# The S5 gate of a hybrid decoder trunk: last block's GELU behind the heads' Sigmoids, unfolding by two engines, gate products of the last block last

## The chip, the cores and the metric

One Trainium2 chip, one core. The metric is the device time of one execution, in microseconds, as the median of three runs. PE is TensorE, DVE VectorE, ACT ScalarE, POOL GpSimd, SP the queue that issues most DMAs.

## The reference

The reference is a decoder trunk of two layers, 512 positions by 1024 channels. The change lies in layer 0, whose mixer has two parallel parts behind one input projection: S5 (512 channels, a complex diagonal recurrence) and HGRN2 (four heads of 128 channels, gated linear attention). Cut to what matters:

```
z = h @ ev_w_in;  u, hq, hf, hi, hg = split(z)
# S5: states over time, then
y   = gelu(Re(C @ states) + d * u)                 # 512 x 512
y_a = y * sigmoid(y @ w_glu + b_glu)               # the S5 gate
# HGRN2, per head
query = silu(hq); forget = lb + (1 - lb) * sigmoid(hf); key = (1 - lb) * sigmoid(-hf)
o   = chunk_gated_linear(query, key, hi, log(forget))
y_b = rms_norm(o) * silu(hg)
mixed = concat(y_a, y_b) @ ev_w_out
```

Then come the residual, a norm with modulation, a SwiGLU FFN, and a second layer with gated linear attention (GLA), another FFN and the last norm. All is float32.

## The kernel before, in words

**Number format.** A float32 product is made of three products of a high and a low part: `split` (line 258) and `wsplit` (line 246) write a high part on ACT and the rest, a difference, on DVE. `proj` (line 269) issues three matmuls for each block of 128 input channels into one PSUM tile of 128 x 512.

**S5.** The 512 channels are four blocks of 128. `s5_block` (line 768) works one block: ACT folds the block so that four time steps share a column (`U`), PE projects it (`vps`), DVE and POOL rotate and scan (`rz...`), and PE forms the output `yp`: for each of four groups j three matmuls of 128 columns (each is recorded as two passes). The output is still folded. Line 813 unfolds it with 16 ACT copies, one for each j and each of four time steps, from 32 partitions of `yp` to every fourth column of `yf`.

**Gate.** `gelu` (line 1080) applies the function to all four `yf`. `s5_glu` (line 816) loads and splits the gate's weights, splits the four `yf` into `yr`, and for each of four output tiles makes 12 matmuls into `ps`, in the order of the input blocks, then a Sigmoid on ACT, a product with `yf` on POOL and a split. Its results `ys` are the first four input blocks of the output projection `out_first` (line 885, tiles `op`).

**Heads.** `hg_fq` (line 1031) projects query and forget gate of one head (`hq`, `hf`); their Sigmoids, and DVE's product for the query (line 1046), read the PSUM tiles. `hg_g` (line 1055) does the output gates of two heads (`hg`). `core` (line 444) is the recurrence of one head in seven levels (`dgp`, `lv`), `hg_outs` norms and gates the heads' outputs (`y_h`).

**PSUM.** Eight banks: four buffers `mm` (`mm_ps`), two `a`, two `b` (`ps_a`, `ps_b`). Buffers of one kind go round in program order; a new tile waits until all readers of the one that had its buffer are done. Head 3's `hq` and `hf`, the two `hg` tiles and then the four gate tiles take the four `mm` buffers in this order. `vps`, `yp` and the fold of the modulation (`ada_run`, line 192, `fold`) use `b`.

**What sets the order.** The program is written in one order (lines 1084 to 1104). A planner with a model of the engines then fixes each engine's queue; it can put work that is written later ahead of work that would wait. ACT's functions with tables are the exception: `tact` (line 91) chains them in program order and puts a table load where the set changes (`sigmoid`, `gelu` and others are different sets). Copies and Squares are in every set. The modulation of later stages is summed on DVE step by step (`ada_run`), with its weights loaded on SP.

Of the kernel before, what the change touches and what calls it, by code (L numbers as in the profile page):

```python
# [13 lines left out]
AF = mybir.ActivationFunctionType  # L14
# [3 lines left out]
P = 128  # L18
D = 1024
T = 512  # L20
# [21 lines left out]
def trunk(  # L42
# [10 lines left out]
    out = out[0]  # L53
# [11 lines left out]
    def tt(name, tag, shape=(P, T), dtype=F32):  # L65
        return tp.tile(list(shape), dtype, tag=tag, name=name, bufs=SLOTS[tag])
# [7 lines left out]
    def mm_ps(name, shape=(P, T)):  # L74
        return pm.tile(list(shape), F32, tag="mm", name=name)

    def ps_a(name, shape=(P, T)):
        return pa.tile(list(shape), F32, tag="a", name=name)

    def ps_b(name, shape=(P, T)):  # L80
        return pa.tile(list(shape), F32, tag="b", name=name)

    V, A, G, PE = nc.vector, nc.scalar, nc.gpsimd, nc.tensor

    def act(o, i, f, **kw):
        return A.activation(out=o, in_=i, func=f, **kw)  # L86
# [4 lines left out]
    def tact(o, i, f, **kw):  # L91


        def queue(new):
            if table["last"] is not None:
                tc.add_manual_dep(new.ins, table["last"].ins.name, order, reason="table sets in order")
            table["last"] = new

        if table["set"] != TABLES[f]:
            table["set"] = TABLES[f]  # L100
            queue(A.preload_act_table_set(TABLES[f]))
        ins = act(o, i, f, **kw)
        queue(ins)
        return ins

    def ttv(e, o, a, b, op):
        e.tensor_tensor(out=o, in0=a, in1=b, op=op)  # L107
# [133 lines left out]
    def wraw(src, nk, name, cols=P):  # L241
        raw = wp.tile([P, nk, cols], F32, tag="raw", name=f"raw_{name}", bufs=3)
        nc.sync.dma_start(out=raw, in_=src.rearrange("(k p) n -> p k n", p=P))
        return raw

    def wsplit(raw, nk, name, cols=P, e=nc.vector):
        hi = wp.tile([P, nk, cols], F32R, tag="whi", name=f"whi_{name}", bufs=3)
        act(hi, raw, AF.Copy)
        lo = wp.tile([P, nk, cols], F32R, tag="wlo", name=f"wlo_{name}", bufs=3)
        ttv(e, lo, raw, hi.bitcast(F32), ALU.subtract)  # L250
        return hi, lo
# [6 lines left out]
    def split(e, src, name, th, tl):  # L258
        hi = tt(f"hi_{name}", th, dtype=F32R)
        lo = tt(f"lo_{name}", tl, dtype=F32R)  # L260
        act(hi, src, AF.Copy)
        ttv(e, lo, src, hi.bitcast(F32), ALU.subtract)
        return hi, lo
# [5 lines left out]
    def proj(ps, ws, acts, ts=slice(0, T), ks=None):  # L269

        n = len(ws)
        for i, ((hi, lo), (ah, al)) in enumerate(zip(ws, acts, strict=True)):
            if ks and i not in ks:
                continue
            PE.matmul(ps, lhsT=hi, rhs=ah[:, ts], start=(i == 0), stop=False)  # L275
            PE.matmul(ps, lhsT=hi, rhs=al[:, ts], start=False, stop=False)  # L276
            ins = PE.matmul(ps, lhsT=lo, rhs=ah[:, ts], start=False, stop=(i == n - 1))  # L277
        return ins
# [238 lines left out]
    def in_step(*runs):  # L517

        runs = list(runs)
        while runs:  # L520
            runs = [r for r in runs if next(r, runs) is not runs]
# [246 lines left out]
    def s5_block(q, uT, mats, rot):  # L768

        rho = prm[3]  # L770
        Km, Wn, (Wr, Wi) = mats
        cosT, sinT = rot
        shp = [P, 4, P]
        U = tt(f"U{q}", "X" if q < 3 else "s", (P, 4, P))
        for j in range(4):
            for s in range(4):
                r = 3 - s
                act(U[32 * r : 32 * r + 32, j, :], uT[32 * j : 32 * j + 32, s:T:4], AF.Copy)
        vps = []
        for i in range(2):  # L780
            ps = ps_b(f"vps{q}{i}", (P, 4, P))
            for j in range(4):
                PE.matmul(ps[:, j, :], lhsT=Wn[i][:, j, :], rhs=U[:, j, :], start=True, stop=True)
            vps.append(ps)
        t = [tt(f"rz{q}{z}", "s", shp) for z in "abcd"]
        ttv(V, t[0], vps[0], cosT, ALU.mult)
        ttv(V, t[1], vps[1], sinT, ALU.mult)
        ttv(V, t[2], vps[1], cosT, ALU.mult)
        ttv(V, t[3], vps[0], sinT, ALU.mult)
        ttv(V, t[0], t[0], t[1], ALU.add)  # L790
        ttv(G, t[2], t[2], t[3], ALU.subtract)
        z = [t[1], t[3]]
        for i in range(2):
            for j in range(4):
                V.tensor_tensor_scan(
                    out=z[i][:, j, :], data0=rho[:, q * 4 + j : q * 4 + j + 1].to_broadcast([P, P]),
                    data1=t[2 * i][:, j, :], initial=0.0, op0=ALU.mult, op1=ALU.add)

        ttv(V, t[0], z[0], cosT, ALU.mult)
        ttv(G, t[2], z[1], sinT, ALU.mult)  # L800
        ttv(V, t[0], t[0], t[2], ALU.subtract)
        ttv(V, z[0], z[0], sinT, ALU.mult)
        ttv(G, z[1], z[1], cosT, ALU.mult)
        ttv(V, z[0], z[0], z[1], ALU.add)
        yp = ps_b(f"yp{q}", (P, 4, P))
        for j in range(4):
            PE.matmul(yp[:, j, :], lhsT=Km[:, j].rearrange("p t c -> p (t c)"), rhs=U[:, j, :], start=True, stop=False)
            PE.matmul(yp[:, j, 1:], lhsT=Wr[:, j, :], rhs=t[0][:, j, 0 : P - 1], start=False, stop=False)
            PE.matmul(yp[:, j, 1:], lhsT=Wi[:, j, :], rhs=z[0][:, j, 0 : P - 1], start=False, stop=True)
        yf = tt(f"yf{q}", "r")  # L810
        for j in range(4):
            for s in range(4):
                act(yf[32 * j : 32 * j + 32, s:T:4], yp[32 * s : 32 * s + 32, j, :], AF.Copy)
        return yf

    def s5_glu(yf):
        wg = []
        for i in range(2):
            w = wsplit(wraw(s5_w_glu[0, i * 2 * P : (i + 1) * 2 * P, :], 2, f"wg{i}", T), 2, f"wg{i}", T, V)
            wg += [tuple(z[:, k, :] for z in w) for k in range(2)]  # L820
        yr = [split(V, y, f"yr{k}", "s", "s") for k, y in enumerate(yf)]
        res = []
        for m in range(4):
            ps = mm_ps(f"glu{m}")
            proj(ps, [tuple(z[:, m * P : (m + 1) * P] for z in w) for w in wg], yr)
            y = tt(f"ys{m}", "s")
            tact(y, ps, AF.Sigmoid, bias=cols2[:, 12 + m : 13 + m])
            ttv(G, y, y, yf[m], ALU.mult)
            res.append(split(V, y, f"ys{m}", "s", "s"))
        return res  # L830
# [119 lines left out]
    for m in range(KT):  # L950
        ps = mm_ps(f"xps{m}")
# [10 lines left out]
    for m in range(KT):  # L962
        ps = (mm_ps if m < 4 else ps_b)(f"xnps{m}")
# [29 lines left out]
    for i in range(2):  # L993
        w = split(V, raw[3][:, 4 * i : 4 * i + 4, :].rearrange("p k n -> p (k n)"), f"u3{i}", "t", "t")
# [19 lines left out]
    def tok_tiles(src, name, f, tag):  # L1014

        os = [tt(f"{name}{i}s", tag, (P, 2, 2 * P)) for i in range(2)]
        f(os, proj_tok(src, h, name))
        return os
# [36 lines left out]
    def hg_g(pr):  # L1055
        c0 = S5W + 3 * 512 + pr * 2 * P
        return tok_tiles(win[:, c0 : c0 + 2 * P], f"hg{pr}", hg_gate, "n")

    def hg_core(hd, os, fq, vt, pst):
        cs_ = slice((hd % 2) * P, (hd % 2 + 1) * P)  # L1060
        return core(os, f"h{hd}", *fq, lambda w: vt[w // 2][:, w % 2, cs_], P, "t", pst, 4 if hd < 2 else 2)

    def hg_out(hd, os, gt, pst):
        cs_ = slice((hd % 2) * P, (hd % 2 + 1) * P)
        return head_out(f"h{hd}", os, lambda w: gt[w // 2][:, w % 2, cs_], P, "r", pst, hd > 1)

    def hg_outs(*runs):
        in_step(*(r for _, r in runs))
        return sum((res for res, _ in runs), [])

    yfs = []
# [5 lines left out]
        if q < 3:  # L1077
            mats.append(s5_mats(q + 1))

    def gelu():  # L1080
        for y in yfs:
            tact(y, y, AF.Gelu_apprx_tanh)

    os = [[] for _ in range(4)]
# [10 lines left out]
    v1 = hg_v(1)  # L1095
    fq2 = hg_fq(2)
    heads += hg_outs(hg_out(0, os[0], g0, ps_a), hg_out(1, os[1], g0, ps_a))
    gelu()
    fq3 = hg_fq(3)
    g1 = hg_g(1)  # L1100
    ys = s5_glu(yfs)
    in_step(hg_core(2, os[2], fq2, v1, ps_a), hg_core(3, os[3], fq3, v1, ps_b))
    heads += hg_outs(hg_out(2, os[2], g1, ps_a), hg_out(3, os[3], g1, ps_b))
# [21 lines left out]
    def gla_qk(hd, i):  # L1125
        c0 = 512 * i + hd * P
        w = wload(win[:, c0 : c0 + P], KT, f"g{'qk'[i]}{hd}")
        return (mm_ps if hd or i else ps_b)(f"g{'qk'[i]}{hd}"), blocks(w)

    qk = [gla_qk(0, i) for i in range(2)]  # L1130
    ps = ps_a("ga1")
# [20 lines left out]
    for hd in range(4):  # L1152
        ps = mm_ps(f"ga2{hd}")
# [12 lines left out]
        for i, z in enumerate((Q, K)):  # L1166
            ps, w = qk[i] if hd == 0 else gla_qk(hd, i)
# [98 lines left out]
```

## Time and profile before

| | us |
|---|---|
| median of three runs | 1331.22 |
| the three runs | 1331.22, 1335.37, 1330.83 |
| the profiled execution, its time | 1336.73 |
| its span | 1334.9 |
| PE busy in it | 1273.0 |
| DVE busy in it | 757.2 |
| ACT busy in it | 513.3 |

The span is what the profile covers of the profiled execution, from its first instruction to its last. Times within it are counted from its start. A matmul that overlaps the next is recorded longer than it delays it: the distance from start to start is what it costs. PEclk is the granted clock of PE, 1.00 for 2.4 GHz and 0.50 for 1.2 GHz. Each engine works its queue in order, so an instruction that waits holds all behind it.

### The profile page before, as it was taken

What the parts mean: (1) busy time and instruction counts of PE and PEld (TensorE: products, weight loads), DVE (VectorE), ACT (ScalarE), POOL (GpSimd) and SP (SyncE); (2) the same over time, 40 slices, a digit from 0 to 9 for tenths busy, and PEclk for the clock granted to TensorE, in tenths of its full rate; (3) what the DMA queues carried; (4) which work ended last, traced back from release to release, by engine and by line L of the source; (5) the groups of instructions that cost most, each with busy time, mean ns of one, the idle gap of its engine ahead of it and who ended that gap; (6) DMA issues with size and microseconds to landing.
All of it is one profiled execution on the core that took longest, in us unless ns stands there. A gap on an engine that the chain in (4) does not pass through costs nothing.

```text
span 1334.9 us, 18302 instructions
## 1 busy us (share of the span) xinstructions
PE 1273.0 (95%) x6973; PEld 1088.8 (82%) x6973; DVE 757.2 (57%) x1420; ACT 513.3 (38%) x939; POOL 138.0 (10%) x151
## 2 busy tenths in 40 slices
PE   7888898799999999999999999999899999999997
PEld 3577887688888888888888999998788888888886
DVE  4787876698755666666345446656743333333344
ACT  5486257534532222222344433433433222222332
POOL 0594440200000000000010000000100000000000
PEclk9899899799999999999999999999999999999999
DMA  8744323156197679876240322214033323333232
GB/s 298 199 121 132 95 79 88 50 142 144 42 222 187 183 191 228 213 200 185 77 145 22 107 67 70 66 49 126 26 110 95 95 77 101 110 100 102 66 93 80
DMA packets 222825, 159.71 MB, mean 120 GB/s; under 512 B 16752, under 2 KB 195248, under 8 KB 222736
## 3 DMA queue, kind: packets, MB, share of 16 engines
q1 hardware_dynamic: 221696, 157.48, 42.5%
q8 instruction: 55, 0.90, 0.3%
q10 hardware_dynamic: 1040, 1.05, 0.3%
q14 instruction: 34, 0.28, 0.1%
HBM read 156.40 MB, written 2.10 MB: 119 GB/s over the span
## 4 chain that ended last, share of the span: by engine, by line
PE 83%; DVE 7%; ACT 6%; DMA 1%; issue 1%; SPq 0%; DVEq 0%; ACTq 0%
PE f L276 18%; PE f L275 18%; PE f L277 18%; ACT yf L86 2%; PE op L275 2%; PE op L276 2%; PE op L277 2%; PE lv_g L466 2%; ACT U L86 1%; PE gr L300 1%; PE gr L301 1%; PE gr L299 1%; PE gv L301 1%; PE gv L300 1%; PE gv L299 1%
## 5 line engine op out<-in xcount | busy, mean ns | idle before, releaser
L275 PE MATMUL f<-hhi_f,whi_f 128*128 128x512 f32 (+1 forms) x736 | 278.4, 381 | 2.2 <-ACT hhi_f L86 2.2
L276 PE MATMUL f<-hlo_f,whi_f 128*128 128x512 f32 (+1 forms) x736 | 279.4, 381 | 0.3 <-DVE hlo_f L116 0.3
L277 PE MATMUL f<-hhi_f,wlo_f 128*128 128x512 f32 (+1 forms) x736 | 278.8, 380 | 0.0
L86 ACT ACTIVATE whi_f<-raw_f 128x1024 fp32r<-128x1024 f32 x88 | 93.4, 1061 | 308.5 <-PE f L276 171.5
L107 DVE TENSOR_TENSOR wlo_f<-raw_f,whi_f 128x1024 fp32r<-128x1024 f32 x88 | 107.7, 1224 | 115.6 <-ACT whi_f L86 115.0
L275 PEld LDWEIGHTS f<-hhi_f,whi_f 128*128 128x128 f32 x736 | 137.5, 188 | 28.7 <-ACT hhi_f L86 2.6
L276 PEld LDWEIGHTS f<-hlo_f,whi_f 128*128 128x128 f32 x736 | 138.1, 188 | 26.9 <-DVE hlo_f L116 0.8
L277 PEld LDWEIGHTS f<-hhi_f,wlo_f 128*128 128x128 f32 x736 | 138.1, 188 | 26.3
L204 DVE SCALAR_TENSOR_TENSOR acc<-ar,cond,acc 128x512 f32<-128x512 f32 x154 | 121.5, 789 | 15.9 <-DMA ar<-in_ada_w_dram 14.4
L277 PE MATMUL f<-hi_g,wlo_c 128*128 128x512 f32 x312 | 121.7, 390 | 0.0
L276 PE MATMUL f<-lo_g,whi_c 128*128 128x512 f32 x312 | 121.6, 390 | 0.0
L275 PE MATMUL f<-hi_g,whi_c 128*128 128x512 f32 x312 | 121.2, 390 | 0.0
L86 ACT ACTIVATE whi_c<-raw_c 128x768 fp32r<-128x768 f32 (+1 forms) x56 | 44.8, 801 | 161.9 <-PE f L276 112.0
L107 DVE TENSOR_TENSOR g<-g,f 128x512 f32<-128x512 f32 x44 | 30.2, 687 | 109.6 <-PE f L277 109.6
L107 DVE TENSOR_TENSOR wlo_c<-raw_c,whi_c 128x768 fp32r<-128x768 f32 (+1 forms) x56 | 50.2, 897 | 64.7 <-ACT whi_c L86 64.7
L275 PEld LDWEIGHTS f<-hi_g,whi_c 128*128 128x128 f32 x312 | 58.6, 188 | 12.1
L277 PEld LDWEIGHTS f<-hi_g,wlo_c 128*128 128x128 f32 x312 | 58.6, 188 | 12.1
L276 PEld LDWEIGHTS f<-lo_g,whi_c 128*128 128x128 f32 x312 | 58.6, 188 | 12.0
L116 DVE SCALAR_TENSOR_TENSOR x<-f,mod,x 128x512 f32<-128x512 f32 (+1 forms) x36 | 24.8, 689 | 43.0 <-PE f L277 43.0
L107 POOL TENSOR_TENSOR na_m<-na_m,nsq_m 128x256 f32<-128x256 f32 x8 | 6.5, 837 | 354.2 <-ACT nsq_m L86 354.2
L300 PE MATMUL gv<-wlo_gv,hhi_m 128*128 128x256 f32 x128 | 36.7, 287 | 0.0
L301 PE MATMUL gv<-whi_gv,hlo_m 128*128 128x256 f32 x128 | 36.6, 286 | 0.0
(664 smaller groups left out, 2627.6 us busy)
## 6 DMA issues: line engine op xcount, KB each, us to landing
raw_f<-in_ffn_w_dram SPq DMA_DIRECT2D x88, 512.0 KB, 3.9
ar<-in_ada_w_dram SPq DMA_DIRECT2D x256, 128.0 KB, 3.6
ar<-in_ada_w_dram SPq DMA_DIRECT2D x64, 256.0 KB, 5.6
raw_c<-in_ffn_w_dram SPq DMA_DIRECT2D x32, 384.0 KB, 3.2
raw_c<-in_ffn_w_dram SPq DMA_DIRECT2D x24, 320.0 KB, 3.2
raw_gv<-in_od_w_in_dram SPq DMA_DIRECT2D x8, 512.0 KB, 4.3
raw_gr<-in_od_w_in_dram SPq DMA_DIRECT2D x8, 512.0 KB, 3.4
raw_o<-in_ev_w_out_dram SPq DMA_DIRECT2D x8, 384.0 KB, 3.5
```

The costliest lines, as they stand in the source:

```text
L86: return A.activation(out=o, in_=i, func=f, **kw)
L107: e.tensor_tensor(out=o, in0=a, in1=b, op=op)
L116: return V.scalar_tensor_tensor(out=o, in0=a, scalar=s, in1=b, op0=op0, op1=op1)
L204: ins = V.scalar_tensor_tensor(out=acc, in0=w, scalar=c_, in1=acc, op0=ALU.mult, op1=ALU.add)
L275: PE.matmul(ps, lhsT=hi, rhs=ah[:, ts], start=(i == 0), stop=False)
L276: PE.matmul(ps, lhsT=hi, rhs=al[:, ts], start=False, stop=False)
L277: ins = PE.matmul(ps, lhsT=lo, rhs=ah[:, ts], start=False, stop=(i == n - 1))
L299: PE.matmul(o, lhsT=ah[:, s], rhs=hi, start=(k == 0), stop=False)
L300: PE.matmul(o, lhsT=ah[:, s], rhs=lo, start=False, stop=False)
L301: PE.matmul(o, lhsT=al[:, s], rhs=hi, start=False, stop=(k == KT - 1))
L466: PE.matmul(ps[0:nk, w, :].rearrange("p (n b) -> p n b", b=b), lhsT=K[:, w * P : w * P + nk], rhs=qv[:, w * nb : (w + 1) * nb, b:], start= ...
```

## The change

Three places are changed. The last S5 block writes its output into two PSUM tiles of two groups each; ACT unfolds the first, DVE the second. The Gelu of the first three blocks stays where it was; that of the last block is written behind the projections of head 3 and of the output gates, so that in the table order it stands behind their Sigmoids. In `s5_glu` all four gate tiles are taken first; their products with blocks 0, 1 and 2 are written for all tiles, and then, tile by tile, those with block 3, the Sigmoid and what follows.

```diff
@@ s5_block
-        yp = ps_b(f"yp{q}", (P, 4, P))
+        n = 2 if q == 3 else 4
+        yps = [ps_b(f"yp{q}{i}", (P, n, P)) for i in range(4 // n)]
         for j in range(4):
-            PE.matmul(yp[:, j, :], lhsT=Km[:, j].rearrange("p t c -> p (t c)"), rhs=U[:, j, :], start=True, stop=False)
-            PE.matmul(yp[:, j, 1:], lhsT=Wr[:, j, :], rhs=t[0][:, j, 0 : P - 1], start=False, stop=False)
-            PE.matmul(yp[:, j, 1:], lhsT=Wi[:, j, :], rhs=z[0][:, j, 0 : P - 1], start=False, stop=True)
+            yp, i = yps[j // n], j % n
+            PE.matmul(yp[:, i, :], lhsT=Km[:, j].rearrange("p t c -> p (t c)"), rhs=U[:, j, :], start=True, stop=False)
+            PE.matmul(yp[:, i, 1:], lhsT=Wr[:, j, :], rhs=t[0][:, j, 0 : P - 1], start=False, stop=False)
+            PE.matmul(yp[:, i, 1:], lhsT=Wi[:, j, :], rhs=z[0][:, j, 0 : P - 1], start=False, stop=True)
         yf = tt(f"yf{q}", "r")
         for j in range(4):
             for s in range(4):
-                act(yf[32 * j : 32 * j + 32, s:T:4], yp[32 * s : 32 * s + 32, j, :], AF.Copy)
+                o, i = yf[32 * j : 32 * j + 32, s:T:4], yps[j // n][32 * s : 32 * s + 32, j % n, :]
+                if j < n:
+                    act(o, i, AF.Copy)
+                else:
+                    V.tensor_copy(out=o, in_=i)
@@ s5_glu
-        for m in range(4):
-            ps = mm_ps(f"glu{m}")
-            proj(ps, [tuple(z[:, m * P : (m + 1) * P] for z in w) for w in wg], yr)
+        pss = [mm_ps(f"glu{m}") for m in range(4)]
+        wm = [[tuple(z[:, m * P : (m + 1) * P] for z in w) for w in wg] for m in range(4)]
+        for ps, ws in zip(pss, wm):
+            proj(ps, ws, yr, ks=range(3))
+        for m, ps in enumerate(pss):
+            proj(ps, wm[m], yr, ks=(3,))
             y = tt(f"ys{m}", "s")
@@ order of the work
-    def gelu():
-        for y in yfs:
+    def gelu(qs):
+        for y in yfs[qs]:
             tact(y, y, AF.Gelu_apprx_tanh)
...
-    gelu()
+    gelu(slice(0, 3))
     fq3 = hg_fq(3)
     g1 = hg_g(1)
+    gelu(slice(3, 4))
     ys = s5_glu(yfs)
```

## Rows read from the trace of the kernel before

**Rows 1.** The page's first part: busy us, share of the span, instructions.
```profile
PE 1273.0 (95%) x6973; PEld 1088.8 (82%) x6973; DVE 757.2 (57%) x1420; ACT 513.3 (38%) x939; POOL 138.0 (10%) x151
```
**Rows 2.** Chain of waits, 215 to 350 us: start, us, engine, tile, line.
```profile
242.80 0.39 ACT yf L86
...
250.38 0.52 ACT yf L86
250.92 1.28 ACT L101
252.21 0.61 ACT hq L86
252.84 0.70 DVE hq L107
253.58 0.80 PE glu L275
```
**Rows 3.** Busy by stretch: start:end, length, PE, PEld, DVE, ACT, POOL, clock, DMA.
```profile
202.21:204.22 2.01, 2.01 (x20) 2.01 (x19) 2.01 (x3) 0.89 (x4) 0.00 (x0) 1.00 0.21 61
235.47:238.08 2.61, 0.61 (x6) 0.41 (x4) 2.61 (x4) 0.84 (x1) 1.94 (x2) 1.00 0.00 0
238.08:242.60 4.52, 4.40 (x22) 4.21 (x23) 4.07 (x7) 0.00 (x0) 0.00 (x0) 0.62 0.35 102
242.60:246.10 3.50, 3.50 (x32) 3.32 (x30) 1.28 (x3) 3.21 (x9) 0.00 (x0) 1.00 0.92 249
246.10:253.58 7.48, 0.01 (x1) 0.00 (x0) 2.58 (x17) 7.35 (x21) 0.00 (x0) 0.68 0.01 2
253.58:258.87 5.29, 5.29 (x12) 4.13 (x13) 5.19 (x13) 4.04 (x14) 3.04 (x2) 0.50 0.00 0
263.56:266.28 2.72, 2.72 (x13) 2.25 (x12) 0.67 (x2) 1.24 (x3) 1.34 (x2) 1.00 0.23 60
```
**Rows 4.** Instructions of PE in order of time: start, us; in brackets idle before and releaser.
```profile
214.52 0.39 PE L277 MATMUL hf<-hhi_m,wlo_hf 128*128 128x512 f32 x1
...
228.34 0.95 PE L210 MATMUL fold<-ind,acc 128*128 128x4 f32 x8
...
235.35 0.28 PE L301 MATMUL hg<-whi_hg,hlo_m 128*128 128x256 f32 x1
...
238.08 0.49 PE L808 MATMUL yp<-rz3a,Wd0z 128*128 128x127 f32 x2 [2.01 <-DVE rz3a L107]
...
268.10 1.95 PE L452 MATMUL dgp_h<-hq,hk 128*128 128x128 f32 x16
```
**Rows 5.** The same of ACT.
```profile
232.91 0.49 ACT L86 ACTIVATE kT_h<-kht_h 128x384 f32<-128x384 f32 x1 [6.86 <-PE kht_h L492]
...
242.80 6.41 ACT L86 ACTIVATE yf<-yp 32x128 f32<-32x128 f32 x16 [6.29 <-PE yp L809]
...
255.62 0.69 ACT L86 ACTIVATE hi_yr<-yf 128x512 fp32r<-128x512 f32 x1
```
**Rows 6.** The same of DVE.
```profile
227.28 0.68 DVE L107 TENSOR_TENSOR lo_yr<-yf,hi_yr 128x512 fp32r<-128x512 f32 x1
227.88 1.76 DVE L107 TENSOR_TENSOR rz3a<-rz3a,rz3b 128x512 f32<-128x512 f32 x1
...
239.69 0.28 DVE L503 COPY S<-st_h 128x128 f32<-128x128 f32 x1
...
250.41 0.17 DVE L113 TENSOR_SCALAR hnv<-ss 128x4 f32<-128x4 f32 x1 [6.10 <-ACT y_h L86]
```
**Rows 7.** The same of POOL.
```profile
227.44 1.66 POOL L107 TENSOR_TENSOR rz3c<-rz3c,rz3d 128x512 f32<-128x512 f32 x1 [30.22 <-DVE rz3d L107]
...
263.62 1.29 POOL L107 TENSOR_TENSOR ys<-ys,yf 128x512 f32<-128x512 f32 x1 [4.75 <-ACT ys L86]
```
**Rows 8.** Busy times by stretch, as rows 3, up to the heads' last level.
```profile
238.60:268.30 29.70, 22.15 (x108) 19.20 (x109) 19.05 (x64) 18.39 (x48) 5.63 (x4) 0.77 0.20 56
268.30:314.30 46.00, 46.00 (x273) 39.44 (x272) 42.62 (x78) 15.45 (x26) 2.60 (x2) 1.00 0.71 176
```

## The prediction

> **What bounds the kernel now.** The page's first part comes first: TensorE (PE) is busy for 95% of the span [rows 1], so only time in which PE stands still, or runs at the lower of its two clocks, can be won. The second view is the chain of waits around the S5 gate [rows 2]. The reader is to see that between 242.80 and 253.58 us no link of it is a matmul: ScalarE (ACT) unfolds the last block's output (16 copies from 242.80), then comes the Gelu, a table load at 250.92, the Sigmoid of head 3's query, VectorE's (DVE) product hq at 252.84, and only then the first gate product. That product reads nothing of hq. It waits for a PSUM buffer: the four `mm` buffers hold hq3, hf3, hg0 and hg2, and their Sigmoids stand behind the last Gelu, since `tact` keeps the functions with tables in program order. The third view, busy times by stretch [rows 3], prices this: 7.48 us with next to no PE work, and behind them 12 gate products in 5.29 us at a granted clock of 0.50, where 12 at 1.00 took 2.72.
>
> The same view shows a smaller hole in front: from 235.47 to 238.08 PE waits about 2 us for the scan results of block 3, and the 22 passes after it take 4.52 us at clock 0.62. In block 2, 18 such passes took 2.01 at full clock (the view counts those at the edges too), so 22 are worth 2.46.
>
> **The change part by part.**
>
> *Sigmoids ahead of the last Gelu.* hf3's last product is at 214.52, and the heads' last one ends at 235.63 [rows 4]; ACT idles 6.86 us before 232.91 and 6.29 us before 242.80 [rows 5]. Into the first go a table load (1.28) and three Sigmoids (0.61 each [rows 2]), 3.1 us; into the second two Sigmoids and the load back to Gelu, 2.5 us. Of the five, the first three free hf3's buffer and, with a DVE product, hq3's. The gate's first tiles thus find their buffers before PE comes for them. The wait of 7.48 goes, and the clock has no reason to fall: 5.29 − 2.72 = 2.57 goes with it. Two table loads are added, 2 × 1.28 = 2.57 on ACT. I cost them at nothing, because the second lies in the 6.29 us in front of the unfolding, and the third, back to Sigmoid, lies between the last Gelu and the first gate Sigmoid, many us apart (below). Exposed, they would cost 2.57.
>
> The Trainium skill (ScalarE: Activation LUTs, What ACT_TABLE_LOAD costs and the rules for authors) speaks against this part: a switch costs about 2.66 us with its drain, and one set should be finished before the next. No drain shows in the row: the Sigmoid follows 0.01 us after the load. By the page's price the term's upper end would be 5.3 and the sum below 5.3 smaller; by where the loads lie it stays nothing.
>
> *Unfolding from two PSUM tiles.* ACT keeps 8 copies of about 0.40 (16 in 6.41 [rows 5]) and can begin when half the passes are done, not at 242.80. DVE takes 8. The trace has no DVE copy with this strided output. The nearest row is the DVE copy from PSUM of 128 columns, 0.28 [rows 6]; ACT's 0.40 is the other end. So 8 cost 2.2 to 3.2, and I take 2.2. DVE idles 6.10 us before 250.41 [rows 6], which covers them. Even if the passes end no earlier than 242.60, yf3 stands at about 245, and Gelu (0.52 [rows 2]), the split on ACT (0.69 [rows 5]) and on DVE (0.68 [rows 6]) are done at about 247. Without the cover of the next step this chain would be the next wait.
>
> *Gate products of blocks 0 to 2 first, block 3 last.* No matmul is added: 36 products need no yf3, 36 × 0.227 = 8.2 us at full clock. PE after 242.60 has the heads' outputs (3.50 [rows 3]) and these 8.2, so it asks for block 3's split at about 254, some 7 us after it is there. Behind a tile's last product stand Sigmoid (0.61), GpSimd's (POOL) product 1.29 [rows 7] and the split on ACT (0.69) and DVE (0.68), 3.3 us, and the four tiles now come bunched. Cover: nine products of the other tiles (2.0 us) and the 1.95 us of dgp, which already stands behind the gate at 268.10 [rows 4]; one split tile then feeds 12 products (2.7 us) of four output tiles, against 1.3 per tile on POOL. No new wait of size.
>
> *The hole before block 3.* The first two tiles have buffers by then, and 12 products for blocks 0 and 1 (2.7 us) could fill the 2 us and keep the clock up. At most 2.0 + (4.52 − 2.46) = 4.1 is gained, at least nothing, if the queue has them behind block 3. One DVE product more (0.68) in front of block 3's chain could also cost that much. I take 2.0, half.
>
> *The second `ps_b` buffer.* yp's two tiles hold both. The fold of the modulation, now at 228.34 [rows 4] in the middle of the heads' products, then waits for a half that is unfolded, some 243 to 245. Its readers are the residuals of the output projection, far behind. The next sum of `ada_run`, in the one `acc` buffer, and its loads on the SP queue start later with it; they are read at the norm behind that projection. I cost this at nothing; a fold that the queue has too early makes PE wait for the unfolding, some 2 us.
>
> *DVE.* It worked 19.05 of the 29.70 us from 238.60 to 268.30, and 42.62 of the 46.00 after that [rows 8]. With PE's gains of 7.48 + 2.57 + 2.0 = 12.05 the first stretch is 17.7 long and is asked for 19.05 + 2.2 = 21.3. The 3.6 us too many go into the next stretch, which has 3.4 free, not all of it usable. I charge 1.5.
>
> Sum: 7.48 + 2.57 + 2.0 − 1.5 = 10.5 us. The profiled run took 1336.73 (span 1334.9): 1326.2 for it. It lies 5.5 above the median of the three runs, 1331.22, so I forecast 1331.22 − 10.5 = **1320.7**. Its own range, gains of 8 to 13.5, is 1317.7 to 1323.2.
>
> **Rivals.** *A, DVE becomes the wall.* For it: 92% busy in the following stretch, and operations that grow while POOL works. rz3a<-rz3a,rz3b took 1.76 [rows 6], beside POOL's product of 1.66 [rows 7]; an operation of that shape just before it, lo_yr, took 0.68, so a collision is 1.08; the gate's four POOL products now come in a row, while DVE splits. Four collisions are 4.3: 21.3 + 4.3 = 25.6 of DVE work after 238.60, a gain of 29.7 − 25.6 = 4.1, to about 1327; with two collisions 6.3, 1325. Against it: some of this work can slip to where the output projection ends. The Trainium skill states this as a rule (SBUF — State Buffer, Who interferes with whom): a DVE instruction with two SBUF inputs and a GpSimd instruction that reads SBUF exclude one another, and the later one waits until the other ends. The trace agrees: rz3a ended 0.5 us after POOL did.
>
> *B, the hole is filled too*, and DVE keeps up: 7.48 + 2.57 + 4.1 = 14.2, to 1317.
>
> *C, the change doesn't do what it says.* PE's queue asks for tile 2 or 3, whose buffers wait for hg's products on DVE behind block 3's scans, ahead of other work, and the wait only changes its name. Left are the 3.2 us of the shorter unfolding: 1328. Against it: hg's inputs are done at 235.63, and DVE's scan chain ends by 238.6.
>
> *D, slower.* Place: the start of heads 2 and 3, dgp at 268.10. Their chain of levels runs to 314.3 and uses DVE for 42.62 of 46.00 us. If DVE comes to it later than now, because the copies (2.2), the collisions (4.3) and the earlier products stand ahead of heads 0 and 1's outputs, the output projection moves up and ends early, and PE then waits for the levels. The price is the delay: up to 6.5, 1337.7. It decides from the point where dgp starts later than 268.1. Against it: DVE idles 10.65 of the 29.70 us before, which would all have to be lost first.
>
> **How the numbers follow.** Forecast 0.46, A 0.24, B 0.11, C 0.10, D 0.09. The measurement cannot tell 0.5%, 6.7 us, from no change. Faster holds forecast, B and a little under half of A: 0.46 + 0.11 + 0.11 = 0.68. Same holds the rest of A and C: 0.23. Slower is D: 0.09. The range runs from 1316, under B with the whole hole and a little more, to 1330, over C; outside lie D and tails.
>
> **What would show it.** Right: no PE wait over 1 us between 238 and 258; clock 1.00 for all 48 gate products; the last gate product at 255 to 259, dgp with it; table loads at about 226, 237 and 246. The step on the hole is judged by the granted clock of block 3's passes. The DVE term is wrong if DVE has idle time left before dgp, or if PE waits for DVE between dgp and the end of the levels. The whole is wrong if the first gate product still waits for hq or hg, or if dgp stays at 268.

## The result, and the profile after

The change makes the kernel slower: 1342.21 us (median of 12 runs, 1339.41 to 1345.92) against 1333.76 for the kernel before on the same chip (1329.99 to 1339.31), a ratio of 1.0066 with a 95% interval of 1.0053 to 1.0080, or 8.8 us. The forecast was 1320.7, faster. Its profiled execution took 1341.38 (span 1339.6).

The page's first part, and from its fourth the shares of the chain by engine:

```profile
PE 1273.0 (95%) x6973; PEld 1089.1 (81%) x6973; DVE 765.2 (57%) x1428; ACT 513.2 (38%) x933; POOL 141.5 (11%) x151
```
```profile
PE 78%; DVE 11%; ACT 4%; DMA 3%; issue 2%; POOL 1%; SPq 0%; DVEq 0%; ACTq 0%; POOLq 0%
```

Beside [rows 1] nothing seems to have happened. The waits of PE between 200 and 360 us (us in total, times, longest) show more:

```profile
PE lv_h L466 <- DVE e_h L107: 5.6, 3, 4.7
PE op L276 <- DVE lo_ys L107: 5.1, 1, 5.1
PE kht_h L492 <- DVE S L116: 2.3, 1, 2.3
PE kht_h L492 <- ACT sc_h L86: 2.1, 1, 2.1
PE or L275 <- ACT hi_y_h L86: 2.0, 2, 1.1
PE op L275 <- ACT hi_ys L86: 1.3, 1, 1.3
```

The wait of 7.48 us for hq [rows 2] is gone; 5.1 behind the gate and 4.7 at the end of the heads' levels have come, both for DVE. The timeline of PE (start, us, operation, count, idle time before it) places them:

```profile
230.00 0.40 PE L275 MATMUL glu<-hi_yr,whi_wg 128*128 128x512 f32 x1
232.93 0.55 PE L492 MATMUL kht_h<-cs,hk 128*128 128x128 f32 x3 [2.30 <-DVE S L116]
...
245.37 0.61 PE L512 MATMUL o_h<-hv00s,sc_h 128*128 128x128 f32 x4
...
253.48 0.39 PE L277 MATMUL glu<-hi_yr,wlo_wg 128*128 128x512 f32 x1
...
255.51 1.08 PE L275 MATMUL op<-hi_ys,whi_o 128*128 128x512 f32 x2 [1.25 <-ACT hi_ys L86]
261.66 0.79 PE L276 MATMUL op<-lo_ys,whi_o 128*128 128x512 f32 x1 [5.07 <-DVE lo_ys L107]
...
270.40 1.05 PE L452 MATMUL dgp_h<-hq,hk 128*128 128x128 f32 x8
...
310.49 1.51 PE L466 MATMUL lv_h<-e_h,hk 128*96 128x64 f32 x8 [4.73 <-DVE e_h L107]
...
325.71 0.73 PE L275 MATMUL or<-hi_y_h,hi_or 128*128 128x256 f32 x4 [1.05 <-ACT hi_y_h L86]
```

The gate starts 23.6 us earlier than before and ends 14 us earlier, yet dgp of head 2 starts at 270.40, where before had both heads' at 268.10 [rows 4]. (Head 3's dgp, which takes a `b` buffer, already starts at 249.62, among the gate products.) Head 2 takes one of the two `a` buffers, which come free behind the outputs of heads 0 and 1 (y_h, their transposes and the split of these), and y_h is DVE's work:

```profile
250.30 0.75 DVE L204 SCALAR_TENSOR_TENSOR acc<-ar,cond,acc 128x512 f32<-128x512 f32 x1
250.97 0.16 DVE L113 TENSOR_SCALAR hnv<-ss 128x4 f32<-128x4 f32 x1
...
251.71 0.74 DVE L204 SCALAR_TENSOR_TENSOR acc<-ar,cond,acc 128x512 f32<-128x512 f32 x1
...
252.92 0.74 DVE L204 SCALAR_TENSOR_TENSOR acc<-ar,cond,acc 128x512 f32<-128x512 f32 x1
253.58 1.24 DVE L113 TENSOR_SCALAR hrs<-hnt 128x4 int32<-128x4 int32 x1
...
259.11 1.75 DVE L204 SCALAR_TENSOR_TENSOR acc<-ar,cond,acc 128x512 f32<-128x512 f32 x1
...
261.53 0.74 DVE L204 SCALAR_TENSOR_TENSOR acc<-ar,cond,acc 128x512 f32<-128x512 f32 x1
...
264.40 0.61 DVE L116 SCALAR_TENSOR_TENSOR y_h<-o_h,hrs,hg00s 128x128 f32<-128x128 f32 x2
...
265.64 0.61 DVE L116 SCALAR_TENSOR_TENSOR y_h<-o_h,hrs,hg00s 128x128 f32<-128x128 f32 x2
...
308.93 0.75 DVE L204 SCALAR_TENSOR_TENSOR acc<-ar,cond,acc 128x512 f32<-128x512 f32 x1 [3.07 <-DMA ar<-in_ada_w_dram]
```

Read it from y_h upwards. Five sums of the modulation (acc, 0.74 each, 4.7 us with one that takes 1.75) stand ahead of y_h, four of them behind the first operation of the root's chain (hnv, hnt, hrs). At 308.93 another waits 3.07 us for its load, with the heads' e_h behind it; PE then has nothing to do for 4.73. Busy times by stretch, columns as in rows 3:

```profile
300.00:310.00 10.00, 5.76 (x36) 4.87 (x34) 6.93 (x15) 2.65 (x4) 0.00 (x0) 0.94 1.00 222
310.00:320.00 10.00, 8.06 (x43) 7.11 (x44) 6.26 (x17) 2.16 (x6) 0.00 (x0) 0.50 0.43 120
```

After that wait the granted clock is 0.50 (1.2 GHz): from the levels' end (kht, 314.98) to the first product of the rest of the projection (or) 10.73 us pass; before, from 314.25 to 322.34, 8.09.

**A zero for the clock of the stages.** Times since the span's start mislead here. In a stretch long before the change, 140 to 182 us, the granted clock was 0.88 in the profiled execution of before and 1.00 in that of after, although the traces have the same instructions in the same order up to 218 us. That is most of the 4.65 us by which the last product of the heads' values (hv) lies apart, at 181.46 and 176.81. The profiled executions differ by 4.65 us in all (1336.73 and 1341.38) and the medians by 8.45, so these times are not to be compared as they stand. Below, stages are counted from that product. Before: the second head's dgp at +87.5 (the row at 268.10 holds both heads' 16 passes, so the second head's start some 0.9 us into it), first FFN product (340.55) at +159.1. After: +93.6 and, at 344.05, +167.2. The 8.1 us of loss lie between, and some 6 of them are there at dgp. What PE did from that product to the first FFN product, before and after, columns as in rows 3:

```profile
181.46:340.55 159.09, 142.13 (x896) 124.51 (x894) 125.47 (x285) 82.75 (x199) 28.40 (x23) 0.96 0.41 106
176.81:344.05 167.24, 145.21 (x895) 127.30 (x894) 130.60 (x293) 82.69 (x193) 29.63 (x23) 0.93 0.38 100
```

PE stands still for 17.0 us before and for 22.0 after, and the same products keep it busy 3.1 us longer, at a lower granted clock. So the wait of 7.48 went, and more waiting came than went.

### The profile page after: what moved, and what is told of

Same layout as the page of the kernel before. It is cut to its first block, busy times and chain, and to the rows that moved or that the text cites. A ratio compares the mean times of both kernels' runs of the same rounds, so it can differ in the third digit from the quotient of the medians.

```text
span 1339.6 us, 18308 instructions
## 1 busy us (share of the span) xinstructions
PE 1273.0 (95%) x6973; PEld 1089.1 (81%) x6973; DVE 765.2 (57%) x1428; ACT 513.2 (38%) x933; POOL 141.5 (11%) x151
## 4 chain that ended last, share of the span: by engine, by line
PE 78%; DVE 11%; ACT 4%; DMA 3%; issue 2%; POOL 1%; SPq 0%; DVEq 0%; ACTq 0%; POOLq 0%
PE f L276 18%; PE f L275 18%; PE f L277 18%; DVE acc L204 2%; PE lv_g L466 2%; ACT yf L86 1%; DMA ar<-in_ada_w_dram 1%; PE gr L300 1%; PE gr L301 1%; PE gv L301 1%; PE gr L299 1%; PE gv L300 1%; PE op L276 1%; PE gv L299 1%; PE op L275 1%
```

## The experiments

Theory T, formed on these rows: DVE comes late to heads 0 and 1's outputs, so dgp and everything behind it starts late. Rivals at first: L (the added table loads), the copies moved to DVE, D (the loads of the modulation, later called R). The table has the start of the second head's dgp and the first FFN product, both from the last hv product of the same profile, and the ratio to the kernel before, which ran beside each of them; its median was 1332.86 to 1334.99 there, so ratios are compared, and us below or above before are the ratio's distance from 1 times that median. dgp and FFN come from one execution each.

| kernel | median us | ratio [95%] | dgp | FFN |
|---|---|---|---|---|
| before | 1333.76 | 1 | 87.5 | 159.1 |
| the change | 1342.21 | 1.0066 [1.0053, 1.0080] | 93.6 | 167.2 |
| e1 Gelu order only | 1333.40 | 1.0009 [0.9993, 1.0025] | 87.0 | 159.2 |
| e2 unfolding only | 1331.18 | 0.9989 [0.9975, 1.0003] | 84.0 | 157.1 |
| e3 two tiles, ACT copies | 1341.91 | 1.0059 [1.0036, 1.0082] | 98.5 | 164.7 |
| e4 sums later | 1341.37 | 1.0064 [1.0045, 1.0083] | 87.7 | 166.3 |
| e5 outputs first | 1333.30 | 0.9996 [0.9983, 1.0010] | 83.9 | 158.3 |
| e6 one load | 1338.64 | 1.0037 [1.0022, 1.0052] | 95.0 | 165.8 |
| e7 both | 1335.12 | 1.0008 [0.9997, 1.0020] | 83.9 | 157.7 |
| e8 e2, outputs first | 1334.99 | 1.0000 [0.9981, 1.0018] | 80.8 | 156.2 |
| e9 e7 without sums | 1333.51 | 0.9992 [0.9977, 1.0007] | 84.1 | 158.6 |
| e10 sums pinned | 1330.58 | 0.9971 [0.9955, 0.9986] | 86.0 | 155.5 |
| e11 e5, products on DVE | 1335.31 | 1.0005 [0.9990, 1.0020] | 83.3 | 157.6 |
| e12 e8, three sums a load | 1338.56 | 1.0022 [1.0006, 1.0039] | 107.8 | 161.3 |
| e13 before, sums pinned | 1331.00 | 0.9979 [0.9962, 0.9997] | 87.4 | 158.7 |
| e14 e1, sums pinned | 1333.87 | 0.9994 [0.9977, 1.0010] | 85.2 | 158.8 |
| e15 e2, sums pinned | 1329.40 | 0.9958 [0.9941, 0.9974] | 82.3 | 155.1 |
| e16 e3, sums pinned | 1338.30 | 1.0029 [1.0012, 1.0046] | 91.3 | 162.3 |

**e1, e2, e3: the parts apart.** e1 takes the unfolding of before:

```
-        n = 2 if q == 3 else 4
+        n = 4                        # and all 16 copies by act
```


> The change with its unfolding undone: one PSUM tile, 16 copies on ACT, as before; the Gelu of the last block stays behind the heads' Sigmoids. Theory T (the time behind the gate is set by the moment when VectorE's queue reaches the first eviction of heads 2 and 3, sc_h<-dgp, 271.5 us in the changed kernel and 270.5 before; what PE gains at the gate is waited away behind the projection): without the eight copies that moment comes 4 to 8 us earlier than in the change, so 1330 to 1337 us, 5 to 12 below the change. Rival L (the two added table loads, 2 x 1.28 us, and the late Gelu are the loss): the loads are still there, so no better than the change, 1340 to 1344. Rival D (VectorE is held up by the loads ar of the modulation, 8 us on the chain at 300.75): as slow as the change, within 2 us.

e2 keeps the unfolding and puts all Gelus ahead of the heads' Sigmoids again:

```
-    gelu(slice(0, 3))
+    gelu(slice(0, 4))
...
-    gelu(slice(3, 4))
```


> The change with its Gelu order undone: all four Gelus ahead of the heads' Sigmoids as before, the unfolding split over two PSUM tiles and two engines as in the change. T: the first gate product waits for hq again, some 3 us less than before, and VectorE has 3.2 us of copies more in front of heads 2 and 3; the two about cancel: before's time, -3 to +2 us. Rival L: the loads are gone, so 3 us faster than before. Rival D: between before and the change, nearer to the change.

e3 keeps both and the two tiles, with the 16 copies on ACT:

```
-                if j < n:
-                    act(o, i, AF.Copy)
-                else:
-                    V.tensor_copy(out=o, in_=i)
+                act(o, i, AF.Copy)
```


> The change with all 16 unfolding copies on ACT, from the two PSUM tiles. T: VectorE is rid of 3.2 us in front of heads 2 and 3, all else stays: 2 to 4 us below the change. If the copies on VectorE were the whole loss: 8 to 9 us below it, before's time. Rival L: the change's time, since the loads stay and ACT has more to do. Rival D: the change's time.

Neither half alone costs anything; only together do they. e1 has the same table loads and no loss, so L falls. e3 is as slow as the change, so DVE's copies are not the loss; that it would be 2 to 4 us better was wrong: without them ACT comes later to the squares of o_h, and dgp is 4.9 us later still. The third part of the change needs no run: with the gate products written tile by tile again, as before, the planner gives all five engines the same queues as in the change, instruction for instruction.

**e4: sums held back by count.** No sum for the first four tiles of the projection, four for each later one:

```
+            if l == 0:
+                pace[0] = 0 if m < 4 else 4
```


> The change with the modulation's sums (acc, and the loads ar behind them) held back: none with the first four weight tiles of the output projection, four instead of two with each of the last four. T: six sums, some 5 us with a collision, leave the stretch in front of heads 2 and 3: 3 to 6 us below the change. Rival L: the change's time. Rival D: the loads are bunched in the second half of the projection, so slower than the change, by 2 us or more.

A miss that taught something: dgp came 5.9 us earlier, as T says, but the time stayed. The sums now stood among the last levels and the heads' last outputs, and three of them waited 2.56, 1.12 and 1.08 us for loads between 303 and 315 us. So T does not hold as a statement on this dgp alone: in e4 it is early and the time late, in e3 it is 4.9 us later than in the change at the same time. What counts is all that PE waits for up to the FFN.

**e5, e6, e7: order against loads.** e5 puts the sums and the splits of the gate's output behind heads 0 and 1's outputs in DVE's queue (`last` holds the split lo of head 1's output; ttv returns its instruction):

```
+                    with tc.issue_after(last[0].ins) if last[0] and (l, pieces) == (0, (3,)) else nullcontext():
                         ins = V.scalar_tensor_tensor(out=acc, in0=w, scalar=c_, in1=acc, ...)
...
+            with after(last[0]):
                 res.append(split(V, y, f"ys{m}", "s", "s"))
```


> The change, with VectorE's splits of the gate's output (lo_ys) and the sums of modulation piece 3 queued behind the split of head 1's output, so that nothing of them stands ahead of heads 0 and 1's y_h. Theory T (the loss is that VectorE comes late to heads 0 and 1's outputs, whose PSUM buffer dgp of head 2 needs): last y_h at 257 to 260 instead of 266.8, dgp at 261 to 264 instead of 270.40, the end of the levels (kht) some 7 us before the change's 314.98, the time 5 to 8 us below the change's 1341. Rival R (the loss is the wait of VectorE for a load of the modulation, 305.85 to 308.93, in the middle of the last levels, after which PE works at half clock to about 324): dgp comes earlier, but that wait is as late as before, kht stays within 2 us of 315 and the time within 2 us of the change's.

e6 leaves DVE's queue as it is and takes away what its sums wait for:

```
+                if k == 0 or (l, pieces) != (0, (3,)):
                     wr = wp.tile([P, 2, T], F32, tag="ar", ...)
                     ...
                         nc.sync.dma_start(out=wr[g * r : g * r + r], ...)
```


> The change with the loads of modulation piece 3 left out but for the first; all 16 sums stay, in the same place of VectorE's queue, and read that one tile (so the value of the piece is not the reference's). Theory T: dgp stays at 270.4; only VectorE's wait of 3.07 us goes, the time is at most 3 us below the change's 1341, 1338 or more. Rival R: VectorE's 3.07 and PE's 4.73 us of waiting go, the clock does not fall, so the 10.73 us from kht to the first product of the last heads become about 8.1; kht at 310 to 312, the time 5.5 to 7.5 us below the change's, 1334 to 1336.

e7 has both edits.

> Both edits of the two runs before in one kernel (VectorE's queue in the order of the first; the loads of piece 3 left out but for the first, so that piece's value is not the reference's). If T and R each hold a part, the gains add: 9 to 14 us below the change's 1341, that is 1327 to 1332, below the kernel before by up to 6. If only one holds, the time is that of its own run within 2 us. If VectorE is the wall whatever its order (its work between 220 and 315 us), neither helps by more than 3 us: 1338 or more.

e5 takes back the whole loss: dgp 9.7 us earlier, the ratio at 0.9996. e6 gives 3.9 us (1.0066 to 1.0037), a little more than the 3 that T allows and less than R's 5.5, and dgp stays late. e7 adds nothing to e5, so its sum of gains was wrong: once the outputs are early, no load is late (no sum waits for one between 250 and 330 us in e5). So DVE's order bears the loss; R's wait is a part of it, worth 3.9 us, and goes with it.

**e8, e9: what bounds the rest.** e8 is e2 with e5's order.

> Two PSUM tiles and VectorE's copies kept, all Gelus ahead of the heads' Sigmoids as in the kernel before, and VectorE's queue with heads 0 and 1's outputs ahead of lo_ys and the sums of piece 3. Theory T: y_h of heads 0 and 1 stands at 254 to 258 already without the new order, so only the sums move: 0 to 3 us below the kernel with these two tiles alone (1331.2), 1328 to 1331. Rival R: within 1 us of it.

Its interval covers e2's and before's, so this order gains nothing there. (e15 below pins the sums alone on e2 and has 0.9958: beside the sums, holding the gate's splits back is no gain and seems to cost. e5 against e10 points the same way, 0.9996 and 0.9971, with intervals that overlap. Why is open.) e9 is e7 without 15 of the sums:

```
-                else:
+                elif (l, pieces) != (0, (3,)):
```


> The kernel with outputs first and one load (e7, 1335.1) with 15 of the 16 sums of modulation piece 3 left out as well (its value is not the reference's): 15 x 0.74 = 11.1 us less of VectorE's work, nearly all behind heads 0 and 1's outputs. Theory W (VectorE is the wall from dgp to the end of the levels): the levels end 5 to 10 us earlier and the time is 5 to 9 us below e7's, 1326 to 1330. Rival P (TensorE is: in e7 it is busy for 47.43 of the 47.43 us from dgp to kht): that stretch stays within 1 us, the time within 2 us of e7's.

W falls. Taking 11.1 us of work from DVE moves the ratio by 0.0016, 2.1 us, about the 2 that P allows and far from W's 5 to 9. The levels themselves do end earlier (the heads' kht at 302.10 and 308.19, where e7 has both at 311.54, with dgp 0.8 us later), but PE is full all the while with the projection, so the time stays. In e9's busy times from dgp to the first state product behind the levels PE (first value) works 48.37 of 48.37 us, DVE (third) only 35.09:

```profile
264.93:313.30 48.37, 48.37 (x262) 41.33 (x262) 35.09 (x62) 16.55 (x28) 4.61 (x3) 0.93 0.38 100
```

So behind dgp DVE's amount of work is no wall, and ahead of it the order counts.

**e10: one edit on the change.** Only the first of e5's two edits, the sums.

> The change with the sums of modulation piece 3 alone queued behind the split of head 1's output on VectorE; the splits of the gate's output (lo_ys) stand where the planner puts them, ahead of it. Theory T (sums): what stood ahead of y_h was mainly the sums (five, 4.7 us in all), so this one edit gives most of the 9 us that both orders gave together: 1333 to 1336, and as PE has op products to do while it waits for y_h, perhaps 1 to 2 us below the kernel with both orders (1333.3). Rival (splits): the wait for the gate's output is what delays y_h; the time stays above 1338.

This is faster than before by 3.9 us and than the change by 12.7 (0.9971 against 1.0066), a little more than expected. DVE's timeline of e10:

```profile
255.22 0.17 DVE L115 TENSOR_SCALAR hnv<-ss 128x4 f32<-128x4 f32 x1 [0.40 <-ACT y_h L86]
...
260.16 0.60 DVE L118 SCALAR_TENSOR_TENSOR y_h<-o_h,hrs,hg00s 128x128 f32<-128x128 f32 x2
...
264.76 0.61 DVE L118 SCALAR_TENSOR_TENSOR y_h<-o_h,hrs,hg00s 128x128 f32<-128x128 f32 x2
...
268.74 0.74 DVE L207 SCALAR_TENSOR_TENSOR acc<-ar,cond,acc 128x512 f32<-128x512 f32 x1
269.40 1.28 DVE L109 TENSOR_TENSOR sc_h<-dgp_h,cs 128x512 f32<-128x512 f32 x2
```

From hnv to head 1's y_h (264.76) it is 9.5 us, against 14.7 in the change (250.97 to 265.64).

**e11, e12: two further ideas.** e11 is e5 with the gate products moved from POOL:

```
-            ttv(G, y, y, yf[m], ALU.mult)
+            ttv(V, y, y, yf[m], ALU.mult)
```


> The change with both orders on VectorE's queue (e5, 1333.3) and the four gate products on VectorE instead of POOL. Theory A (collisions with POOL cost about 1 us each): the operations of VectorE beside them shrink from 1.25 to 1.8 us to their 0.15 to 0.75, some 3.5 us, against 4 x 0.68 = 2.7 of products added: VectorE is 0.8 less busy, the last y_h is up to 1 us earlier, the time 0 to 2 us below e5's. Rival (collisions are nothing): VectorE has 2.7 more, the time is 1 to 3 us above e5's.

Inconclusive: the interval overlaps e5's, though the second head's dgp is 0.5 us earlier. e12 is e8 with faster sums upstream:

```
-    pace[:] = 2, 3
+    pace[:] = 3, 3
```


> The kernel with two tiles, VectorE's copies, early Gelus and outputs first (e8, 1335.0 where before has 1333.6), with three instead of two modulation sums for each weight load in the S5 and heads stage, so that 6 to 10 sums of piece 3 move out of the stretch from 260 to 310 us, into 100 to 250, where VectorE is busy for 73 to 77%. W: 3 to 6 us below e8's, and below the kernel before. P: within 2 us of e8's. If the sums get in front of the S5 blocks' chains there: 3 us or more slower.

Nearest to the last of the three outcomes: 3 us slower than e8, with intervals that overlap. The second head's dgp only comes at 288.70; which chain the sums held up is not shown.

**e13 to e16: which part bears e10's gain.** The same pin of the sums, on the kernel before, on e1, on e2 and on e3.

> The kernel before with the same one edit as e10: the sums of modulation piece 3 queued behind the split of head 1's output on VectorE. Theory G (the gate's wait is worth something once VectorE's order lets it through): in the trace of before only two sums stood ahead of y_h, so the edit gives 0 to 1.5 us: 1332 to 1335. Rival O (the order alone bears e10's gain of 4 us): 3 to 4 us below before, 1330 to 1332.

> The change with one PSUM tile and all 16 copies on ScalarE, its Gelu order kept, and the sums pinned as in e10. G: this order of the Gelus removes the wait for the four mm buffers, so it bears 2 to 4 us below before once the sums are out of the way. O: the same as e13 within 1 us. If the unfolding bears the gain: within 1 us of e13 too.

> The change with all Gelus ahead of the heads' Sigmoids (as before), its two PSUM tiles and VectorE's eight copies kept, and the sums pinned as in e10. The two tiles alone (e2) were 1.5 us below before; G: 2 to 4 us below before, as e10; O: as e13 within 1 us.

> The change with all 16 copies on ScalarE, two PSUM tiles kept, and the sums pinned as in e10. VectorE has 3.2 us less, but block 3's gate input stands 3.2 us later. G: within 2 us of e10's, 1329 to 1333; if the eight copies on VectorE are what frees the path: 3 us or more above e10's.

e15 has the lowest ratio: 1329.40, 5.6 us below before, with the two tiles and DVE's eight copies and without the new Gelu order (its interval overlaps e10's and e13's). e14 shows that this order gives nothing even with the sums out of the way, where G expected 2 to 4; e13, with neither part of the change, gains 2.8 (0.4 to 5.1), between G and O. e16 is 7.7 us above e10, so copying on DVE is worth that much here: it frees ACT for the squares (ACT unfolds for 6.44 us in e16 and for 3.20 in e10). In e13 the wait that the change was to remove is still there, whole, as PE's timeline shows:

```profile
240.88 0.61 PE L515 MATMUL o_h<-hv00s,sc_h 128*128 128x128 f32 x4
...
251.63 0.80 PE L278 MATMUL glu<-hi_yr,whi_wg 128*128 128x512 f32 x1 [7.46 <-DVE hq L109]
...
266.11 1.95 PE L455 MATMUL dgp_h<-hq,hk 128*128 128x128 f32 x16
```

And still it is within 0.0008, about 1 us, of e10, which has no such wait (each interval reaches some 2 us to either side). The two profiles, from the last hv product (181.31 in e10, 179.59 in e13) to the first FFN product:

```profile
181.31:336.77 155.46, 142.13 (x895) 124.07 (x894) 127.85 (x293) 82.72 (x193) 29.43 (x23) 0.97 0.43 108
179.59:338.28 158.69, 141.97 (x896) 124.45 (x894) 125.47 (x285) 82.91 (x199) 28.75 (x23) 0.96 0.42 106
```

PE stands still for 13.3 us in e10 and for 16.7 in e13: of the 7.46, 3.4 are left as a gain in these executions. In e15 the same operations read:

```profile
236.88 1.06 PE L515 MATMUL o_h<-hv00s,sc_h 128*128 128x128 f32 x4
...
243.76 0.50 PE L278 MATMUL glu<-hi_yr,whi_wg 128*128 128x512 f32 x1 [2.06 <-DVE hq L109]
...
256.86 1.05 PE L455 MATMUL dgp_h<-hq,hk 128*128 128x128 f32 x8
258.53 1.11 PE L455 MATMUL dgp_h<-hq,hk 128*128 128x128 f32 x8
```

## Why the prediction was wrong

**The step that failed is the first term:** "The wait of 7.48 goes", and 2.57 of clock with it, counted in full as time won because "only time in which PE stands still ... can be won". The wait did go, but PE ran into the next one. Beside the gate ran another chain: last states of heads 0 and 1 (o_h on PE), squares on ACT, root on DVE, y_h, its transposes (yT_h) on PE, dgp. In the trace of before it was not far behind; DVE makes head 1's y_h and PE asks for it here:

```profile
262.44 0.61 DVE L116 SCALAR_TENSOR_TENSOR y_h<-o_h,hrs,hg00s 128x128 f32<-128x128 f32 x2
262.96 0.60 DVE L116 SCALAR_TENSOR_TENSOR y_h<-o_h,hrs,hg01s 128x128 f32<-128x128 f32 x2
```
```profile
267.19 0.38 PE L541 MATMUL yT_h<-cs,y_h 128*128 128x128 f32 x2
```

From 263.56 to 267.19 are 3.6 us. This is an estimate of what an earlier gate alone could win, of the 10.05 counted. In e10, with the sums out of the way, PE does wait for y_h:

```profile
261.34 0.66 PE L544 MATMUL yT_h<-cs,y_h 128*128 128x128 f32 x4 [2.64 <-DVE y_h L118]
```

e10 and e13, without and with the wait, differ by about 1 us in their medians and by 3.2 us at the first FFN product of their profiles. Where the wait is shortened and that chain moves up with it (e15: 2.06 us, dgp at +82.3 against e13's +87.4), the ratio is 0.9958 against 0.9979.

**"No matmul is added" was true and not enough.** The gate products moved ahead of these states in PE's queue. In the change the kht and o_h of heads 0 and 1 (232.93, 245.37) lie among the gate products; counted from the last hv product o_h starts at +68.6 (245.37), in e10 at +68.5 and in e13, whose order there is that of before, at +61.3. That is 7.2 us later. The root then starts 5.2 us later than before (hnv at +74.2 and +69.0) and head 1's y_h 7.8 (+88.8 and +81.0); the rest is DVE's queue. In e10, with o_h as late as in the change, head 1's y_h starts at +83.5. By these readings the late o_h alone does not make the loss, but it takes back much of what the gate had won. No run took the gate products alone out of that place with everything else kept.

**The modulation.** The prediction saw that the fold would wait (228.34 to 246.93) and costed it at nothing, since its readers are far behind. The readers were not the price. The next piece's sums came with it, and the planner put five of them ahead of y_h. Pinning them was worth 12.7 us on the change (e10) and 2.8 on the kernel before (e13), by far the largest effect measured; what comes with it are the missing wait for the load at 308.93 and the clock behind it. This term, put at nothing, is what made the change slower than before.

**The DVE term.** 1.5 us was charged for an overflow of work into the next stretch. e9 shows that the amount was no wall there. The copies took 3.19 us for eight, the upper of the two bounds given, where 2.2 was taken; they cost nothing, on the contrary (e16).

**Right in mechanism:** most of the gate's own steps. From 240 us to the gate's end the granted clock was 1.00, the last product came at 253.48, ahead of the 255 to 259 said, and nothing waited for block 3's split. The table loads lie at 218.10, 230.81 and 247.66, and e1, which has them too, is not slower than before. Block 3 itself came later, not earlier: its unfolding starts at +66.0 (242.84) where before has +61.3 (242.80), since on DVE and on PE other work now stands ahead of it; the products of the other blocks covered that. The hole before block 3 was not won: PE waits 2.30 us for S at 232.93 in its place, and the granted clock from 230 to 240 is 0.83, not 1.00 for all 48 products. Behind the gate PE waits 1.25 us for hi_ys and 5.07 for lo_ys, which "No new wait of size" had excluded. The prediction's own sign, "if dgp stays at 268", called it rightly: 270.40.

**The rivals.** D named the right place and deciding point: dgp later than before, the projection early, PE waiting for the levels. Its price, up to 6.5 us, was too low for the 8.8 measured, since the sums and their loads were not in it. Its 0.09 rested on "DVE idles 10.65 of the 29.70 us before, which would all have to be lost first". That counted work, where a queue in order is delayed by what stands ahead: from hnv to the end of y_h in the change (250.97 to 266.76) DVE is busy for 15.76 of 15.79 us. A's four collisions happened: 1.24, 1.23, 1.75 and 1.23 us for operations that take 0.16, 0.15, 0.74 and 0.15 alone, 4.3 us as worked out. What they cost in time e11 could not resolve. B and C did not occur.

## What to carry to other kernels

Before a wait is counted as won, follow the chain that ends next behind it: from the first operation of the next full stretch (here dgp) back through the buffer it needs, and ask how far that path lies behind the wait. No more than that distance can be won. What is moved earlier on an engine in order stands ahead of something; name that, on every engine, and any filler work (sums, prefetches) whose start hangs on a step that is moved. When an edit that fills a hole makes a kernel slower, try pinning the filler behind the critical operation first: here that one constraint on the order turned 8.8 us of loss into 3.9 of gain.

## What the runs showed of the hardware

**The same waits, two clocks.** The change and e7 have the same instructions in the same order on their compute engines up to 250 us. In both PE waits near 147 us for wlo_hv (1.60 and 1.52 us) and near 156 for sc_h (2.55 and 2.54). Busy times of the change (PE first, granted clock the third value from the end):

```profile
152.00:156.00 4.00, 1.46 (x13) 1.28 (x12) 4.00 (x5) 0.00 (x0) 1.55 (x2) 1.00 0.17 55
156.00:160.00 4.00, 3.99 (x35) 4.00 (x36) 4.00 (x9) 0.60 (x1) 1.49 (x2) 1.00 0.79 210
```

and of e7:

```profile
152.00:156.00 4.00, 1.46 (x12) 1.29 (x11) 4.00 (x5) 0.00 (x0) 1.34 (x1) 0.90 0.24 67
156.00:160.00 4.00, 4.00 (x20) 4.00 (x21) 4.00 (x9) 0.19 (x1) 1.70 (x2) 0.50 0.75 202
```

The same waits left the clock at 1.00 (2.4 GHz) in one and were followed by 0.50 (1.2 GHz), little more than half the products in the stretch, in the other. The last hv product then lies 3.4 us apart (176.81 and 180.23). What decides is not shown. Part of the scatter of 3 to 11 us within each kernel's runs may be this; only profiled executions show it.

**A small operation can be held as long as a large one.** The TENSOR_SCALAR hrs<-hnt at 253.58, of four columns and one input, took 1.24 us beside POOL's product (253.31, 1.48 us) and 0.16 alone. The Trainium skill (SBUF — State Buffer, Who interferes with whom) lists tensor_scalar among the operations that can, where their operands meet its conditions, contend for the port pair shared with GpSimd; the trace agrees, with 1.08 us.

**One late load stops its whole queue.** The sum at 308.93 waited 3.07 us, and e_h, which needs nothing of it, behind it.
